# The first weight tile behind three norms computed before the norm's factor is known

## The chip, the cores and the metric

The kernel runs on one core of one Trainium2 chip. The metric is the device time of one execution in microseconds (us), median of three runs. A profile is taken of a further execution of the same program; its span runs from the first to the last instruction, and its device time is a little longer than the span.

## The reference, cut to what matters

Two decoder layers work on 256 tokens of width 1024. Layer 0 mixes tokens with dilated attention, layer 1 with gated linear attention (GLA); each is followed by a gated feed-forward part. Ahead of each of these four parts stands a norm that is modulated by a vector `c`:

```python
mod = jax.nn.silu(c) @ w_ada[i] + b_ada[i]
sh1, sc1, g1, sh2, sc2, g2 = [m[:, None, :] for m in jnp.split(mod, 6, axis=-1)]
h = rmsnorm(x, norm_mix[i]) * (1.0 + sc1) + sh1
x = x + g1 * y                                  # y: attention or GLA of h
h = rmsnorm(x, norm_ffn[i]) * (1.0 + sc2) + sh2
x = x + g2 * conv_ffn(h, w_up[i], conv_w[i], conv_b[i], w_down[i])
```

GLA takes from `h` the projections q, k (4 heads), v, a low-rank gate `glr` and an output gate r. From `glr` comes `gk = log_sigmoid(glr @ w_gate + b) / 16`, its running sum over chunks of 64 tokens, and three exponentials of that sum, which scale q and k before anything is done with them.

## The kernel before, in words

Activations are stored transposed: 8 tiles of 128 features by 256 tokens (`x`, and `h_hi`, `h_lo`). Every product is made in about full precision from two reduced parts of each operand: `mm3` (lines 171 to 176) issues hi·hi, hi·lo and lo·hi, so a weight tile of 2048 columns (a pair of 128-column blocks for 8 feature tiles) is 48 matmuls of 128 x 256. `split` (155 to 169) loads such a tile with one DMA of 1 MB on SyncE's queue, casts its two halves on ScalarE (`whi`, line 165) and subtracts them on VectorE (`wlo`, line 168). There are four raw buffers and three of each split part.

A norm is: `residual` (271) adds the last products to `x` on VectorE; `add_square` (195) squares on ScalarE and adds up; `rstd_of` (183) sums over features with three matmuls by a constant (line 186), then Ln and Exp on ScalarE (188, 190); `normed` (246) makes for each feature tile `x·(1+scale)·r` on VectorE (250), the hi part with the shift on ScalarE (252) and the lo part on VectorE (253). `all_normed` (265) does this for three of the four norms: ahead of the feed-forward part of layer 0, of GLA, and of the feed-forward part of layer 1. Between the sums and the first product it issues six small matmuls on constants (`keep_warm(6)`, line 263).

The modulation vectors are computed in 48 chunks: `ada_chunk` (129) loads 1 MB and reduces it in two VectorE instructions (138) to two columns of 128. Eight chunks belong to the first norm; the other 40 stand in the list `rest` and `next_ada()` takes the next one at places written into the loops.

`ffn` (541) runs 22 up-projection tiles (`pab`), each followed by a convolution over tokens and a gate, and then 32 down-projection tiles (`pd`). GLA first makes v (`pv`, four tiles), with the low-rank gate after the second (`log_gates`, 614): `glr` (621), four products `z` (625), `nz` (626), Abs, Exp and Ln on ScalarE (630 to 632), `sp` (634) and the running sum `cs` (637) on VectorE, `e_q` and `e_k` (641, 642), `dl` (644), `e_d` (646). Then `states(hd)` (673) for each head: 48 matmuls for q and k into one PSUM bank of the tag "p", of which there are two, then `k_d`, `q_t`, `k_t` (682 to 684) on VectorE, which need the exponentials, and then small matmuls on them (690, 696, 706).

The program is ordered by a scheduler that simulates a timeline; the order on each engine is then fixed. `behind(...)` keeps an instruction after another one on the same engine. Each engine issues strictly in this order.

Of the kernel before, what the change touches and what calls it, by code (L numbers as in the profile page):

```python
# [11 lines left out]
F32 = mybir.dt.float32  # L12
# [6 lines left out]
P = 128  # L19
# [38 lines left out]
def trunk(ctx: ExitStack, tc: tile.TileContext, I, out):  # L58
# [93 lines left out]

    last_load, copied, last_lo = [None], [None], [None]

    def split(src, n, dmas=1, after=((), ())):
        raw = wraw.tile([P, 2048], F32, tag="raw", name="raw")
        for i in range(dmas):
            c = slice(n * i // dmas, n * (i + 1) // dmas)
            last_load[0] = nc.sync.dma_start(raw[:, c], src[:, c])
        hi = wspl.tile([P, 2048], F32R, tag="whi", name="whi")  # L160
        lo = wspl.tile([P, 2048], F32R, tag="wlo", name="wlo")
        for i in range(0, n, n // 2):
            c = slice(i, i + n // 2)
            with behind(*after[i > 0]):
                copied[0] = nc.scalar.copy(hi[:, c], raw[:, c])  # L165
        for i in range(0, n, n // 2):
            c = slice(i, i + n // 2)
            last_lo[0] = nc.vector.tensor_tensor(lo[:, c], raw[:, c], hi[:, c].bitcast(F32), op=ALU.subtract)  # L168
        return hi, lo

    def mm3(ps, a, b, start, stop):
# [4 lines left out]
        return mm(ps, a[1], b[0], start=False, stop=stop)  # L176

    def hpart(name, dt, n=KT):
        return [state.tile([P, T], dt, tag=f"{name}{k}", name=name) for k in range(n)]

    norm_ops = []

    def rstd_of(squares, n=D, tag=None):
        ps = bank("ms", tag)
        for i, sq in enumerate(squares):
            a = mm(ps[:, :T], ones_d, sq, start=(i == 0), stop=(i == len(squares) - 1))
# [3 lines left out]
        norm_ops[:] = a, nc.scalar.activation(r, ln, AF.Exp, scale=-0.5)  # L190
        return r

    sums = {}

    def add_square(kt):

        sq = tmp.tile([P, T], F32, tag="sq", name="sq")
        i = nc.scalar.activation(sq, x[kt], AF.Square)
        part = 0 if kt < 3 else 1 if kt < 7 else 2
        if kt in (0, 3, 7):  # L200
            sums[part] = sq
        else:
            acc = tmp.tile([P, T], F32, tag="sqacc", name="sqacc")
            (nc.gpsimd if kt < 3 else nc.vector).tensor_tensor(acc, sums[part], sq, op=ALU.add)
            sums[part] = acc
        if kt < 6:
            squared[0] = i
# [38 lines left out]
    def normed(l, sub, r, kt):  # L246

        xr = tmp.tile([P, T], F32, tag="xr", name="xr")
        a, sh = mod[l, 3 * sub + 1, kt], mod[l, 3 * sub, kt]
        nc.vector.scalar_tensor_tensor(xr, x[kt], a[:, 0:1], r, op0=ALU.mult, op1=ALU.mult)  # L250
        hi, lo = h_hi[kt][:, :], h_lo[kt][:, :]
        i = nc.scalar.activation(hi, xr, AF.Identity, bias=sh[:, 0:1])  # L252
        j = nc.vector.scalar_tensor_tensor(  # L253
            lo, xr, sh[:, 0:1], hi.bitcast(F32), op0=ALU.add, op1=ALU.subtract
        )
        chain[kt] = chain[7] = i, j
        return h_hi[kt], h_lo[kt]

    def keep_warm(n):

# [1 line left out]
        for i in range(n):  # L262
            mm(ps[:, :P], ones_d, ones_d, start=True, stop=True)

    def all_normed(l, sub):
        r = rstd_of([sums[0], sums[1], sums[2]])
        with behind(norm_ops[0]):
            keep_warm(6)
        return [normed(l, sub, r, kt) for kt in range(KT)]

    def residual(l, sub, kt, ps):
        g = mod[l, 3 * sub + 2, kt]
        i = nc.vector.scalar_tensor_tensor(x[kt], ps, g[:, 0:1], x[kt], op0=ALU.mult, op1=ALU.add)
        if kt < 6:
            squared[1] = i

    def parts(w, at, n=P):
        return w[0][:, at : at + n], w[1][:, at : at + n]
# [49 lines left out]
    for kt in range(KT):  # L328
        with behind(*first):
            term = ada_chunk(0, kt, dmas=1 if kt else 2)  # L330
        h.append(normed(0, 0, r, kt))
        if kt:
            w0.append(split(I["w0"][kt], 15 * P))
        else:
            with behind(chain[0][1]):
                w0.append(split(I["w0"][kt], 15 * P, 2, after=((term,), (chain[0][0],))))
# [178 lines left out]
    def project(src, o, l, sub):  # L515

        ends = []
        for n in range(4):
            w = split(src[n], 2048)
            ps = [bank("py", "ppst"[n])] * 2  # L520
            if n == 3:
                ps[1] = bank("py", "s")
            order = [(kt, i) for kt in range(KT) for i in range(2)]
            if n == 3:
                order.sort(key=lambda x: x[1])
            for kt, i in order:
# [12 lines left out]
    last_pd = [None]  # L539

    def ffn(l):
        h = all_normed(l, 1)
        with tc.tile_pool(name=f"ffn{l}", bufs=2) as pool:
            g_hi = [pool.tile([P, T], F32R, tag=f"ghi{i}", name="ghi", bufs=1) for i in range(NFF)]
            g_lo = [pool.tile([P, T], F32R, tag=f"glo{i}", name="glo", bufs=1) for i in range(NFF)]
            for i in range(NFF):
                with behind(*(squared[:1], chain[3], chain[7])[min(i, 2)]):
                    w = split(I["w_up"][l, i], 2048)
                pab = bank("pab")
                pu = [pab[:, :T], pab[:, T:]]  # L550
                for kt in range(KT):
# [24 lines left out]
            for f2 in range(0, KT, 2):  # L576
                pd = [bank("pd") for _ in range(2)]
                for half, f in ((0, 0), (0, 1), (1, 0), (1, 1)):
                    w = split(I["w_down"][l, f2 + f, half], 11 * P)
                    for j in range(11):  # L580
                        i = 11 * half + j
                        last_pd[0] = mm3(pd[f][:, :T], parts(w, P * j), (g_hi[i], g_lo[i]), i == 0, i == NFF - 1)
                for f in range(2):
# [4 lines left out]
                    if l == 0 and f2 < 6:  # L588
                        next_ada()

    ffn(0)

# [57 lines left out]

    pv = [[bank("pv", tg) for _ in range(2)] for tg in "ps"]
    for n in range(4):
        with behind(*(squared, chain[5], chain[7], glr_copy)[n]):
            w = split(I["w_v_b"][n], 2048)
            if n > 1:
# [15 lines left out]
    o_n = []  # L671

    def states(hd):
        w = split(I["w_qk_b"][hd], 2048)
        pqk = bank("pqk", "p")
        pq, pk = pqk[:, :T], pqk[:, T:]
        for kt in range(KT):
            mm3(pq, parts(w, 2 * P * kt), h[kt], kt == 0, False)
            mm3(pk, parts(w, 2 * P * kt + P), h[kt], False, kt == KT - 1)
        c = slice(T * hd, T * hd + T)  # L680
        q_t, k_t, k_d = (gt([P, T], nm, bufs=2) for nm in ("q_t", "k_t", "k_d"))
        nc.vector.tensor_tensor(k_d, pk, e_d[:, c], op=ALU.mult)
# [80 lines left out]
    output(3, *s3)  # L763
    for n in range(1, 4):
        gate(n)
        if n < 2:
            next_ada()
    o = []
    for n in range(4):
        r = r_g[n // 2][:, 2 * (n % 2) : 2 * (n % 2) + 2, :]  # L770
# [156 lines left out]
```

## Time and profile before

| | |
|---|---|
| median of 3 runs | 803.75 us (802.86, 803.75, 808.61) |
| device time of the profiled execution | 802.44 us |
| its span | 800.7 us |
| mean granted clock of TensorE | 0.995 |
| TensorE busy | 781.9 us, 98% of the span |
| VectorE, ScalarE, GpSimd busy | 643.9, 468.2, 15.2 us |
| bytes moved | 184.72 MB |

In the views, PE is TensorE (PEld its weight loads), DVE VectorE, ACT ScalarE, POOL GpSimd, SP SyncE. A row of the timeline has start and duration in us, engine, line, operation, output<-input, and at its end the engine's idle time before it with what ended that. A row of the windows has the stretch, its length, the busy time of each engine with the number of instructions, the granted clock (PEclk), the DMA share and GB/s.

### The profile page before, as it was taken

How to read it: one execution, taken by the hardware profiler on the slowest of the kernel's cores; microseconds unless marked ns; L12 is line 12 of the kernel's file. 1: busy time of each engine (PE TensorE's matmuls, PEld its weight loads, DVE VectorE, ACT ScalarE, POOL GpSimd, SP SyncE). 2: the span in 40 equal slices, each digit the busy share in tenths (PEclk: the TensorE clock that was granted, in tenths of full speed). 3: DMA queues.
4: the chain of work that ended last, by engine and by line, in shares of the span. 5: the costliest groups of instructions: out<-in, count | busy, mean ns of one | idle time of the engine just before them, and what ended most of it. 6: DMA issues, size and time to landing. Idle time of an engine off the chain costs nothing.

```text
span 800.7 us, 15941 instructions
## 1 busy us (share of the span) xinstructions
PE 781.9 (98%) x6486; PEld 753.3 (94%) x6486; DVE 643.9 (80%) x1150; ACT 468.2 (58%) x869; POOL 15.2 (2%) x40
## 2 busy tenths in 40 slices
PE   7999999999999999999999999999999999999997
PEld 5999999999999989999999998889998999999997
DVE  6988978879778759999997877785468999988552
ACT  5556555555555546776765545744566866666442
POOL 1000000000000010000000100000010000000100
PEclk9899999999999999999999999999999999999999
DMA  8998577585685825886647793973343777644531
GB/s 343 418 334 298 202 280 278 202 329 197 248 312 200 301 85 204 301 301 223 240 162 249 268 332 127 366 261 108 106 156 109 275 269 248 251 141 159 181 110 53
DMA packets 32183, 184.72 MB, mean 231 GB/s; under 512 B 5804, under 2 KB 7340, under 8 KB 15470
## 3 DMA queue, kind: packets, MB, share of 16 engines
q1 hardware_dynamic: 32110, 183.70, 63.9%
q8 instruction: 51, 0.84, 0.4%
q14 instruction: 22, 0.18, 0.1%
HBM read 182.59 MB, written 1.10 MB: 229 GB/s over the span
## 4 chain that ended last, share of the span: by engine, by line
PE 89%; DVE 5%; DMA 3%; ACT 2%; issue 1%; SPq 0%; ACTq 0%; DVEq 0%
PE pab L176 10%; PE pab L175 10%; PE pab L174 10%; PE pqk L174 7%; PE pqk L175 6%; PE pqk L176 6%; PE pd L176 5%; PE pd L175 5%; PE pd L174 5%; PE pv L174 3%; PE pv L175 3%; PE pv L176 3%; DVE wlo L168 2%; PE py L175 2%; PE py L174 2%; PE s L367 2%
## 5 line engine op out<-in xcount | busy, mean ns | idle before, releaser
L168 DVE TENSOR_TENSOR wlo<-raw,whi 128x1024 fp32r<-128x1024 f32 (+2 forms) x274 | 295.8, 1107 | 55.6 <-ACT whi L165 54.8
L165 ACT CAST whi<-raw 128x1024 fp32r<-128x1024 f32 (+2 forms) x274 | 248.1, 954 | 152.4 <-PE pab L175 50.6
L174 PE MATMUL pab<-hhi,whi 128*128 128x256 f32 x704 | 194.0, 277 | 1.5 <-ACT hhi L252 1.5
L175 PE MATMUL pab<-hlo,whi 128*128 128x256 f32 x704 | 193.9, 276 | 0.5 <-DVE hlo L253 0.5
L176 PE MATMUL pab<-hhi,wlo 128*128 128x256 f32 x704 | 194.0, 276 | 0.4 <-DVE wlo L168 0.4
L174 PEld LDWEIGHTS pab<-hhi,whi 128*128 128x128 f32 x704 | 132.0, 188 | 2.2 <-ACT hhi L252 1.9
L175 PEld LDWEIGHTS pab<-hlo,whi 128*128 128x128 f32 x704 | 132.0, 188 | 0.9 <-DVE hlo L253 0.9
L176 PEld LDWEIGHTS pab<-hhi,wlo 128*128 128x128 f32 x704 | 132.0, 188 | 0.8 <-DVE wlo L168 0.8
L174 PE MATMUL pqk<-hhi,whi 128*128 128x256 f32 x448 | 123.5, 287 | 3.7 <-ACT hhi L252 3.2
L175 PE MATMUL pqk<-hlo,whi 128*128 128x256 f32 x448 | 125.0, 283 | 0.0
L176 PE MATMUL pqk<-hhi,wlo 128*128 128x256 f32 x448 | 124.9, 283 | 0.0
L138 DVE CUSTOM_DVE_ANT_0 ada_raw<-ada_raw,c_bc 128x1024 f32<-128x1024 f32 x96 | 113.5, 1218 | 4.5 <-DMA ada_raw<-in_w_ada 4.4
L176 PE MATMUL pd<-ghi,wlo 128*128 128x256 f32 x352 | 98.0, 280 | 0.6 <-DVE wlo L168 0.6
L175 PE MATMUL pd<-glo,whi 128*128 128x256 f32 x352 | 98.1, 280 | 0.0
L174 PE MATMUL pd<-ghi,whi 128*128 128x256 f32 x352 | 97.7, 279 | 0.0
L174 PEld LDWEIGHTS pqk<-hhi,whi 128*128 128x128 f32 x448 | 83.7, 191 | 5.5 <-ACT hhi L252 3.7
L175 PEld LDWEIGHTS pqk<-hlo,whi 128*128 128x128 f32 x448 | 85.0, 190 | 0.4
L176 PEld LDWEIGHTS pqk<-hhi,wlo 128*128 128x128 f32 x448 | 84.9, 190 | 0.2
L176 PEld LDWEIGHTS pd<-ghi,wlo 128*128 128x128 f32 x352 | 65.8, 187 | 0.8 <-DVE wlo L168 0.8
L175 PEld LDWEIGHTS pd<-glo,whi 128*128 128x128 f32 x352 | 66.0, 188 | 0.0
L174 PEld LDWEIGHTS pd<-ghi,whi 128*128 128x128 f32 x352 | 65.9, 188 | 0.0
L560 ACT ACTIVATE r<-pab,small 128x256 f32<-128x256 f32 x88 | 48.5, 559 | 11.7 <-DVE r L563 11.3
(184 smaller groups left out, 1248.2 us busy)
## 6 DMA issues: line engine op xcount, KB each, us to landing
ada_raw<-in_w_ada SPq DMA_DIRECT2D x47, 1024.0 KB, 6.7
raw<-in_w_up SPq DMA_DIRECT2D x44, 1024.0 KB, 5.2
raw<-in_w_down SPq DMA_DIRECT2D x32, 704.0 KB, 4.2
raw<-in_wqk SPq DMA_DIRECT2D x18, 1024.0 KB, 7.2
raw<-in_wv SPq DMA_DIRECT2D x14, 768.0 KB, 4.6
raw<-in_w SPq DMA_DIRECT2D x7, 960.0 KB, 6.6
raw<-in_w_out_a SPq DMA_DIRECT2D x4, 1024.0 KB, 6.9
raw<-in_w_v_b SPq DMA_DIRECT2D x4, 1024.0 KB, 6.7
```

What stands on the lines that cost most here:

```text
L138: nc.vector.tensor_tensor_reduce(w, w, c_bc, op0=ALU.mult, op1=ALU.add, scale=1.0, scalar=0.0, accum_out=dot,)
L165: copied[0] = nc.scalar.copy(hi[:, c], raw[:, c])
L168: last_lo[0] = nc.vector.tensor_tensor(lo[:, c], raw[:, c], hi[:, c].bitcast(F32), op=ALU.subtract)
L174: mm(ps, a[0], b[0], start=start, stop=False)
L175: mm(ps, a[0], b[1], start=False, stop=False)
L176: return mm(ps, a[1], b[0], start=False, stop=stop)
L367: mm(s[:, 0:n], q[0][a][:, r].rearrange("p a b -> p (a b)"), k[0][b][:, 0:n], start=(i == 0), stop=(i == 2))
L560: nc.scalar.activation(r, u[:, :T], AF.Identity, scale=cw[2], bias=col(C_CB + 44 * l + f))
```

## The change

With r the norm's factor per token, `h = x·(1+scale)·r + shift`. So a product of a weight with h is r times the product with `x·(1+scale)`, plus the product with the shift, which is the same for every token. After the change the first weight tile behind each of the three norms is multiplied with `x·(1+scale)`, and the shift stands in a 257th column (a 258th is zero) of the same operand. When r is there, `whole` multiplies 256 columns of the sums by r and adds the 257th.

For this, `scale(l, sub, kt)` writes hi and lo parts of `x·(1+scale)` into the tiles that later hold h, right after each residual (one instruction on ScalarE, one on VectorE for each feature tile); `shift_columns` writes the shift's two parts (eight instructions of one column on each of the two engines, for each norm); the h tiles grow by 32 columns, cleared at the start on GpSimd. The products of the first two feature tiles go ahead of the sums over features, the other six behind them, in the place of `keep_warm(6)`. In the feed-forward parts this tile is the first of the up-projection; at GLA it is q and k of head 0, kept in `qk0`, so that `states(0)` has no product of its own. The second weight tile is split at chosen places of the norm.

Modulation chunks move: in the up-projections 6 become 3 (layer 0) and 4 become 0 (layer 1); the v loop has 3 instead of 2, the gates 4 instead of 2, and the down-projection of layer 1 has 4 instead of 0. In all they stay 40.

```diff
+    def shift_columns(l, sub):
+        for kt in range(KT):
+            hi, lo = (z[kt][:, T : T + 1] for z in (h_hi, h_lo))
+            with behind(*chain[7]):
+                nc.scalar.copy(hi, mod[l, 3 * sub, kt])
+                nc.vector.tensor_tensor(lo, mod[l, 3 * sub, kt], hi.bitcast(F32), op=ALU.subtract)
+
+    def scale(l, sub, kt):
+        a, hi, lo = mod[l, 3 * sub + 1, kt], h_hi[kt][:, 0:T], h_lo[kt][:, 0:T]
+        i = nc.scalar.activation(hi, x[kt], AF.Identity, scale=a[:, 0:1])
+        j = nc.vector.scalar_tensor_tensor(lo, x[kt], a[:, 0:1], hi.bitcast(F32), op0=ALU.mult, op1=ALU.subtract)
+        scaled[kt] = i, j
...
-    def all_normed(l, sub):
-        r = rstd_of([sums[0], sums[1], sums[2]])
+    def all_normed(l, sub, tags, second):
+        ps = [bank("early", t) for t in tags]
+        def products(tiles):
+            for kt in tiles:
+                for s in range(2):
+                    mm3(ps[s][:, 0:TS], parts(early[0], 2 * P * kt + P * s), (h_hi[kt][:, 0:TS], h_lo[kt][:, 0:TS]),
+                        kt == 0, kt == KT - 1)
+        products(range(2))
+        r = rstd_of([sums[0], sums[1], sums[2]], tag="p")
         with behind(norm_ops[0]):
-            keep_warm(6)
-        return [normed(l, sub, r, kt) for kt in range(KT)]
+            products(range(2, KT))
+        def whole(s, out):
+            dot = tmp.tile([P, 1], F32, tag="dot", name="dot", bufs=4)
+            nc.scalar.copy(dot, ps[s][:, T : T + 1])
+            nc.vector.tensor_tensor(out, ps[s][:, 0:T], r, op=ALU.mult)
+            nc.scalar.activation(out, out, AF.Identity, bias=dot[:, 0:1])
+            return out
+        h = [normed(l, sub, r, kt) for kt in range(KT)]
+        early[1] = split(second, 2048, after=(scaled[6][:1], chain[0][:1], last_x, chain[2][1:]))
+        return h, whole
...
     def project(src, o, l, sub):
+        shift_columns(l, 1)
...
+            if n == 3:
+                with behind(*scaled[3]):
+                    early[0] = split(I["w_up"][l, 0], 2048)
             for i in range(2):
                 residual(l, sub, 2 * n + i, ps[i][:, T * i : T * i + T])
                 add_square(2 * n + i)
+                scale(l, 1, 2 * n + i)
...
     def ffn(l):
-        h = all_normed(l, 1)
+        h, whole = all_normed(l, 1, "st", I["w_up"][l, 1])
...
-                if i % (3, 5)[l] == 2 and i < 20:
-                    with behind(*chain[7]):
+                if l == 0 and i % 7 == 3:
+                    with behind(last_lo[0]):
                         next_ada()
...
+                    if l == 1 and (half, f) == (0, 0):
+                        next_ada()
...
-    h = all_normed(1, 0)
+    h, whole = all_normed(1, 0, "tt", I["w_v_b"][0])
...
     for n in range(4):
+        if n == 0:
+            w = early[1]
+            with behind(*chain[7]):
+                qk0 = gt([P, 2, T], "qk0")
+                for s in range(2):
+                    whole(s, qk0[:, s, :])
+        else:
+            with behind(*((), chain[5], chain[7], glr_copy)[n]):
+                w = split(I["w_v_b"][n], 2048)
+            with behind(last_lo[0]):
                 next_ada()
...
     def states(hd):
+        if hd == 0:
+            pq, pk = qk0[:, 0, :], qk0[:, 1, :]
+        else:
+            w = split(I["w_qk_b"][hd], 2048)
...
     for n in range(1, 4):
         gate(n)
-        if n < 2:
-            next_ada()
+        next_ada()
```

More of the change, by code (lines that the diff above doesn't have):

```diff
@@ L153, in trunk, with split @@
     last_load, copied, last_lo = [None], [None], [None]
-    def split(src, n, dmas=1, after=((), ())):
+    def split(src, n, dmas=1, after=((), (), (), ())):
         raw = wraw.tile([P, 2048], F32, tag="raw", name="raw")
@@ L167, in split @@
             c = slice(i, i + n // 2)
-            last_lo[0] = nc.vector.tensor_tensor(lo[:, c], raw[:, c], hi[:, c].bitcast(F32), op=ALU.subtract)
+            with behind(*after[2 + (i > 0)]):
+                last_lo[0] = nc.vector.tensor_tensor(lo[:, c], raw[:, c], hi[:, c].bitcast(F32), op=ALU.subtract)
         return hi, lo
@@ L178, in hpart @@
     def hpart(name, dt, n=KT):
-        return [state.tile([P, T], dt, tag=f"{name}{k}", name=name) for k in range(n)]
+        return [state.tile([P, T + 32], dt, tag=f"{name}{k}", name=name) for k in range(n)]
     norm_ops = []
@@ L191, in rstd_of @@
         return r
-    sums = {}
+    sums, last_sum, last_x = {}, [], []
     def add_square(kt):
@@ L203, in add_square @@
             acc = tmp.tile([P, T], F32, tag="sqacc", name="sqacc")
-            (nc.gpsimd if kt < 3 else nc.vector).tensor_tensor(acc, sums[part], sq, op=ALU.add)
+            last_sum[:] = [(nc.gpsimd if kt < 3 else nc.vector).tensor_tensor(acc, sums[part], sq, op=ALU.add)]
             sums[part] = acc
@@ L250, in normed @@
         nc.vector.scalar_tensor_tensor(xr, x[kt], a[:, 0:1], r, op0=ALU.mult, op1=ALU.mult)
-        hi, lo = h_hi[kt][:, :], h_lo[kt][:, :]
+        hi, lo = h_hi[kt][:, 0:T], h_lo[kt][:, 0:T]
         i = nc.scalar.activation(hi, xr, AF.Identity, bias=sh[:, 0:1])
@@ L256, in normed @@
         chain[kt] = chain[7] = i, j
-        return h_hi[kt], h_lo[kt]
+        return h_hi[kt][:, 0:T], h_lo[kt][:, 0:T]
+    TS = T + 2
+    for z in h_hi + h_lo:
+        nc.gpsimd.memset(z[:, T:].bitcast(F32), 0.0)
+    early, scaled = {}, {}
+    def shift_columns(l, sub):
[9 more added lines that the diff above has]
+        scaled[kt] = i, j
     def keep_warm(n):
@@ L263, in keep_warm @@
             mm(ps[:, :P], ones_d, ones_d, start=True, stop=True)
-    def all_normed(l, sub):
-        r = rstd_of([sums[0], sums[1], sums[2]])
-        with behind(norm_ops[0]):
-            keep_warm(6)
-        return [normed(l, sub, r, kt) for kt in range(KT)]
+    def all_normed(l, sub, tags, second):
[7 more added lines that the diff above has]
+        r = rstd_of([sums[0], sums[1], sums[2]], tag="p")
+        with behind(norm_ops[0]):
+            products(range(2, KT))
[8 more added lines that the diff above has]
+        return h, whole
     def residual(l, sub, kt, ps):
         g = mod[l, 3 * sub + 2, kt]
-        i = nc.vector.scalar_tensor_tensor(x[kt], ps, g[:, 0:1], x[kt], op0=ALU.mult, op1=ALU.add)
+        with behind(*(last_sum if kt == 7 else ())):
+            i = nc.vector.scalar_tensor_tensor(x[kt], ps, g[:, 0:1], x[kt], op0=ALU.mult, op1=ALU.add)
         if kt < 6:
             squared[1] = i
+        last_x[:] = [i]
     def parts(w, at, n=P):
@@ L335, in trunk @@
             with behind(chain[0][1]):
-                w0.append(split(I["w0"][kt], 15 * P, 2, after=((term,), (chain[0][0],))))
+                w0.append(split(I["w0"][kt], 15 * P, 2, after=((term,), (chain[0][0],), (), ())))
             with behind(copied[0]):
@@ L546, in ffn @@
             for i in range(NFF):
[L547 to L551, printed above, removed]
+                w = early.get(i)
+                if i > 1:
+                    with behind(*chain[7]):
+                        w = split(I["w_up"][l, i], 2048)
+                if i == 0:
+                    with behind(*chain[7]):
+                        pu = [whole(s, pool.tile([P, T], F32, tag="u", name="u")) for s in range(2)]
+                else:
+                    pab = bank("pab")
+                    pu = [pab[:, :T], pab[:, T:]]
+                for kt in range(KT if i else 0):
                     for s in range(2):
@@ L576, in ffn @@
             for f2 in range(0, KT, 2):
+                if (l, f2) == (0, 4):
+                    shift_columns(1, 0)
                 pd = [bank("pd") for _ in range(2)]
@@ L582, in ffn @@
                         last_pd[0] = mm3(pd[f][:, :T], parts(w, P * j), (g_hi[i], g_lo[i]), i == 0, i == NFF - 1)
+                if (l, f2) == (0, 6):
+                    with behind(*scaled[3]):
+                        early[0] = split(I["w_qk_b"][0], 2048)
                 for f in range(2):
@@ L587, in ffn @@
                         nc.scalar.mul(x[f2 + f], x[f2 + f], col(C_NFIN + f2 + f))
-                    if l == 0 and f2 < 6:
-                        next_ada()
+                    if l == 0:
+                        scale(1, 0, f2 + f)
+                        if f2 < 6:
+                            next_ada()
     ffn(0)
@@ L652, in trunk @@
     for n in range(4):
-        with behind(*(squared, chain[5], chain[7], glr_copy)[n]):
-            w = split(I["w_v_b"][n], 2048)
-            if n > 1:
+        if n == 0:
+            w = early[1]
+            with behind(*chain[7]):
+                qk0 = gt([P, 2, T], "qk0")
[5 more added lines that the diff above has]
+            with behind(last_lo[0]):
                 next_ada()
@@ L673, in states @@
     def states(hd):
[L674 to L679, printed above, removed]
+        if hd == 0:
+            pq, pk = qk0[:, 0, :], qk0[:, 1, :]
+        else:
+            w = split(I["w_qk_b"][hd], 2048)
+            pqk = bank("pqk", "p")
+            pq, pk = pqk[:, :T], pqk[:, T:]
+            for kt in range(KT):
+                mm3(pq, parts(w, 2 * P * kt), h[kt], kt == 0, False)
+                mm3(pk, parts(w, 2 * P * kt + P), h[kt], False, kt == KT - 1)
         c = slice(T * hd, T * hd + T)
@@ L765, in trunk @@
         gate(n)
-        if n < 2:
-            next_ada()
+        next_ada()
     o = []
```

## The prediction

> **What bounds the kernel now.** I read the page's first part, then the windows of single stages, then the waits of PE, then the timeline where those waits stand.
>
> ```profile
> span 800.7 us, 15941 instructions
> PE 781.9 (98%) x6486; PEld 753.3 (94%) x6486; DVE 643.9 (80%) x1150; ACT 468.2 (58%) x869; POOL 15.2 (2%) x40
> ```
>
> PE is the bound; 18.8 us of the span are its idle time. The device time of this execution is 802.44 us, 1.74 more than the span and 1.31 below the median of the three runs, 803.75. Three windows show how full the stages are (up-projection and down-projection of layer 0, the output projection of layer 1):
>
> ```profile
> 310.00:420.00 110.00, 110.00 (x973) 110.00 (x972) 106.86 (x186) 78.87 (x138) 0.00 (x0) 1.00 0.71 252
> 422.00:485.00 63.00, 62.44 (x530) 62.23 (x530) 47.57 (x75) 31.59 (x55) 2.23 (x2) 1.00 0.81 288
> 585.00:605.00 20.00, 20.00 (x179) 20.00 (x178) 12.85 (x22) 11.04 (x19) 2.08 (x2) 1.00 0.43 152
> ```
>
> The up-projection has no hole: one matmul each 113 ns (110.00/973), a tile of 48 in 5.4 us. DVE is 97% full there, yet PE never waits for it, so taking modulation chunks out of that stage gains nothing. The down-projection runs at 118 ns (62.44/530) with matmuls of the same shape; I come back to this. The output projection leaves DVE 7 of 20 us free. So the change can only gain where PE stands: around the norms.
>
> ```profile
> 297.45 1.03 PE L186 MATMUL ms<-sqacc,ones_d 128*128 128x256 f32 x4
> 298.69 0.70 PE L186 MATMUL ms<-sq,ones_d 128*128 128x256 f32 x2 [0.22 <-ACT sq L198]
> ...
> 299.94 0.42 ACT L190 ACTIVATE rstd<-ln 128x256 f32<-128x256 f32 x1
> 300.39 1.28 DVE L250 SCALAR_TENSOR_TENSOR xr<-x_all,mod,rstd 128x256 f32<-128x256 f32 x3 [2.26 <-ACT rstd L190]
> ...
> 301.58 0.88 DVE L253 SCALAR_TENSOR_TENSOR hlo<-xr,mod,hhi 128x256 fp32r<-128x256 f32 x2
> ```
>
> From the first sum at 297.45 PE does 1.73 us of sums, then warming matmuls and waits until the first h tile at 301.47. The windows of its products from there tell how slowly they begin (the first of the feed-forward part, the second of GLA's v, whose sums start at the time of the third row):
>
> ```profile
> 301.47:306.00 4.53, 4.08 (x29) 3.54 (x29) 0.00 (x0) 0.00 (x0) 1.00 0.00 0
> ...
> 489.48:494.50 5.02, 5.01 (x22) 4.14 (x23) 0.00 (x0) 0.00 (x0) 1.00 0.01 3
> ```
>
> ```profile
> 485.52 1.03 PE L186 MATMUL ms<-sqacc,ones_d 128*128 128x256 f32 x4
> ```
>
> Feed-forward norm: 306.00 - 297.45 = 8.55 us, less 1.73 of sums, less 29 x 0.113 = 3.3 of products: 3.5 us lost. The norm of layer 1 has the same form, 3.5. GLA: 489.48 - 485.52 - 1.73 = 2.2, and from then on PE is full (22 products at 228 ns). In all 9.2 us: the most that the change can gain.
>
> One more wait matters, because the change moves work around it: PE waits in GLA until the exponentials of the gate have scaled k.
>
> ```profile
> 509.35 1.99 PE L625 MATMUL z<-glr,w_g 16*128 16x256 f32 x8
> ...
> 510.89 1.99 ACT L165 CAST whi<-raw 128x1024 fp32r<-128x1024 f32 x2
> ...
> 516.70 1.07 ACT L632 ACTIVATE ea<-ea 128x1024 f32<-128x1024 f32 x1
> 517.80 1.23 DVE L634 SCALAR_TENSOR_TENSOR sp<-nz,ea 128x1024 f32<-128x1024 f32 x1 [0.26 <-ACT ea L632]
> 518.95 1.22 DVE L168 TENSOR_TENSOR wlo<-raw,whi 128x1024 fp32r<-128x1024 f32 x1
> 520.08 2.28 DVE L637 TENSOR_TENSOR_SCAN cs<-keep,sp 128x1024 f32<-128x1024 f32 x1
> 522.40 1.06 ACT L641 ACTIVATE e_q<-cs 128x1024 f32<-128x1024 f32 x1 [2.75 <-DVE cs L637]
> 524.54 1.22 DVE L138 CUSTOM_DVE_ANT_0 ada_raw<-ada_raw,c_bc 128x1024 f32<-128x1024 f32 x1
> 526.83 2.35 DVE L168 TENSOR_TENSOR wlo<-raw,whi 128x1024 fp32r<-128x1024 f32 x2
> ...
> 529.10 0.41 DVE L682 TENSOR_TENSOR k_d<-pqk,e_d 128x256 f32<-128x256 f32 x1
> 529.57 0.44 PE L690 MATMUL kdt<-ident,k_d 128*128 128x128 f32 x2 [1.44 <-DVE k_d L682]
> 530.23 0.71 PE L696 MATMUL a<-q_t,k_t 128*128 128x128 f32 x4 [0.22 <-DVE k_t L684]
> ```
>
> The chain from `z` to `k_d` takes 19.75 us. Meanwhile PE has the rest of v and the products of two heads (96 matmuls), which fill both PSUM banks of the tag "p"; then it stands for 1.44 and 0.22 us. This chain is covered to within 1.7 us, with nothing to spare.
>
> **The change part by part.** The order that the changed program is built with is fixed, so I use it for what stands where.
>
> *Feed-forward norms.* Twelve early products go ahead of the sums: 1.4 us, longer than the residual and the square need, so the sums no longer wait. After the sums follow 36 products, 4.1 us. The factor r comes about 1.0 us after the last sum (rows 298.69 and 299.94: 300.36 - 299.39). What is late next is h for the second tile: h may only be written when r is there, and from then to the end of that tile's products there are 4.1 + 5.4 - 1.0 = 8.5 us, in which DVE has 16 norm instructions at 0.43 (1.28/3, 0.88/2), 6.9 us, the second half of this tile's wlo and both of the next one's at 1.2 each: 10.5 us. So 2.0 of the 3.5 us remain as waits for hlo and wlo; gain 1.5 for each of the two norms (bounds 0 and 3.5: the order may let DVE hold up everything, or nothing).
>
> *GLA's norm.* The v products take 12 x 0.228 = 2.7 us for each feature tile, DVE 0.9; no wait is left: gain 2.2 (lower bound 1). Sum of the three norms 5.2 (1 to 9.2).
>
> *Added work.* `scale` adds per norm 8 instructions to ACT and to DVE, nearest row hlo, 0.44: 3.5 us each. Their cover is the idle DVE of the projections ahead (7 of 20 us; 15 of 63). Without that cover each would come in front of a residual; that is a rival below. Shift columns, `whole`, clearing at the start (POOL is busy 2%): nothing on PE's path; above nothing by the same cover. Early products have 258 columns instead of 256:
>
> ```profile
> L367 PE MATMUL s<-k,q 128*128 128x258 f32 x48 | 10.4, 315 | 0.0
> L367 PE MATMUL s<-k,q 128*128 128x256 f32 x24 | 5.4, 292 | 0.0
> ```
>
> By columns 144 x 1 ns = 0.1 us, by these means 144 x 23 ns = 3.3; the means mix in what follows each, so I take 0.2.
>
> *The gate's chain.* Head 0's products are made at the norm, so PE's cover behind `z` is now the rest of v and heads 1 and 2: again 96 matmuls in the two "p" banks, no more. But the chain gets longer. On DVE a second modulation chunk stands between `sp` and `cs` (2.3 us: 526.83 - 524.54), and `q_t`, `k_t` are issued ahead of `k_d` (0.7). On ACT four more weight casts stand between `nz` and the Ln, since the splits now run one head further ahead: 2 x 1.99 = 4.0 us, and some column copies, 0.2. Sum 7.2. ACT sits idle only behind the Ln (2.75 before `e_q`), so casts ahead of it aren't hidden. Bounds: 2.3 if all ACT work fell into gaps, 9 if a chunk's load also delays a weight in the full DMA queue:
>
> ```profile
> 500.00:510.00 10.00, 10.00 (x55) 8.43 (x54) 7.64 (x10) 4.88 (x7) 0.00 (x0) 1.00 0.96 381
> ```
>
> PE stands 1.7 + 7.2 = 8.9 us in one piece at `a`; behind it in PE's order wait all other heads and the gates, whose work is then done later, not saved.
>
> *The clock.* The trace shows once what a hole does:
>
> ```profile
> 21.63 1.01 PE L174 MATMUL pqk<-hhi,whi 128*128 128x256 f32 x3 [2.70 <-ACT hhi L252]
> ```
>
> ```profile
> 20.00:21.00 1.00, 0.00 (x0) 0.00 (x0) 1.00 (x3) 0.00 (x0) 0.00 (x0) 0.95 0.93 385
> 21.00:24.00 3.00, 2.37 (x9) 2.37 (x10) 3.00 (x7) 2.30 (x4) 0.00 (x0) 0.50 1.02 423
> ...
> 27.00:28.00 1.00, 1.00 (x7) 1.00 (x7) 1.00 (x3) 0.57 (x2) 0.00 (x0) 0.63 1.03 418
> ```
>
> After 2.70 us without work the granted clock is 0.50 from 20.9 to 27.7, 6.1 us of it after work is back: half of that, 3.1 us, is lost if PE is dense, half as much if it is mostly waiting on short chains as behind `a`. I take 2.4 (0 if the hole stays short). The Trainium skill, "TensorE: Matmul & The Clock Gate", Part 1, says that one idle window of about 3.4 us halves the clock and one busy window of that length restores it, windows running freely. The row agrees in kind; by the rule alone the return would cost 1.7 us instead of 2.4. It also speaks against the change where `keep_warm` goes, but there the 36 products keep PE busy.
>
> *Moved chunks* elsewhere stay under PE: in the down-projection of layer 1 DVE has room as in layer 0 (47.57 of 63).
>
> Sum: -5.2 + 7.2 + 2.4 + 0.2 = +4.6 us on 802.44: **807.0 us**.
>
> **The rivals.**
>
> *A. The gain arrives, the hole doesn't grow.* Casts and chunk slip into waits of the chain that are there anyway (before `sp` 0.26, before `e_q` 2.75). Then 802.44 - 9.2 + 2.3 = 795.5. For it: ACT is busy only 58%. Against it: the row of `e_q` has its slack behind the Ln, not ahead.
>
> *B. The up-projections fall to the slower pace.* The same matmul takes 113 ns in one stage and 118 in another, at a granted clock of 1.00 in both, so something that the stages' rows don't name sets it. The up-projection now follows early products instead of a halt, and reads h tiles 1152 bytes apart. If its 42 remaining tiles ran at 118: 2016 x 4.7 ns = 9.5 us, 816.5; one layer alone 811.7. It decides with the first tile behind each norm. Against it: both layers ran at 113.
>
> *C. The early block is late itself.* If `scale` delays the residual, the square or the wlo of the early tile, PE waits ahead of the block as it did behind the sums, and the norms gain nothing: 807.0 + 5.2 = 812.2. For it: two DVE instructions more for each pair of output tiles, in front of the last wlo. Against it: DVE's free time in those projections.
>
> **How the numbers follow.** Forecast 0.55, A 0.12, B 0.20, C 0.13. The forecast's own range is 802 to 812 (its bounds without the extremes together). The whole range goes to 799, which keeps the near half of A, and to 816, B in nearly both layers. About 1% is what a measurement of this kernel tells from no change, 8 us: 795.7 to 811.8. Faster by more is half of A, 0.06. Slower by more is three quarters of B, half of C and the forecast's upper end (0.04): 0.26. The rest, 0.68, is within 1%.
>
> **What would show each step.** Right: no warming matmuls, 48 early products for each norm with no wait over 0.3 us among them; waits of 1 to 2.5 us for hlo and wlo in the second and third tiles; PE waiting 7 to 10 us for `k_t` or `k_d`, a granted clock of 0.50 after it; two reductions between `sp` and `cs`. Wrong: a wait under 3 us there (A), 118 ns in the up-projections (B), waits ahead of the early products (C).

## The result, and the profile after

The changed kernel takes 814.09 us (median of 7 runs, 810.79 to 816.19) against 803.75: a ratio of 1.0125, 95% interval 1.0103 to 1.0146. A second comparison later gave 1.0123 (1.0104 to 1.0142). It is slower by 10 us. The prediction said 807.0, 799 to 816: the sign and the range held, the sum was 7 us too small by the medians. The time lies above the forecast's own range of 802 to 812, and the prediction had put 0.68 on a change within 1%. The profiled execution took 811.51 us, 9.07 more than that of before (802.44); the terms below are held against this difference, of which +4.6 was forecast.

The page's first part, with the idle time of PE now 24.8 us of the span:

```profile
span 809.7 us, 16040 instructions
PE 784.9 (97%) x6450; PEld 757.2 (94%) x6450; DVE 660.0 (82%) x1204; ACT 483.3 (60%) x929; POOL 16.0 (2%) x56
```

PE is idle 6 us longer, and busy 3 us longer with 36 matmuls fewer. Both halves need a cause. The waits of PE (time in total, times, longest) name the first:

```profile
PE a L769 <- DVE k_t L757: 8.8, 1, 8.8
PE pd L177 <- DVE wlo L169: 1.6, 1, 1.6
PE pab L177 <- DVE wlo L169: 1.0, 2, 0.5
PE pab L176 <- DVE hlo L254: 0.5, 2, 0.2
```

One stall of 8.8 us stands out, at `a`, the small matmuls of `q_t` and `k_t`; in the tiles behind the norms 1.5 us is left in all (the rows of `pab`). The timeline of the chain that ends in it:

```profile
515.82 1.99 PE L688 MATMUL z<-glr,w_g 16*128 16x256 f32 x8
...
528.17 1.23 DVE L697 SCALAR_TENSOR_TENSOR sp<-nz,ea 128x1024 f32<-128x1024 f32 x1 [0.64 <-ACT ea L695]
529.31 1.22 DVE L138 CUSTOM_DVE_ANT_0 ada_raw<-ada_raw,c_bc 128x1024 f32<-128x1024 f32 x1
...
530.45 1.22 DVE L138 CUSTOM_DVE_ANT_0 ada_raw<-ada_raw,c_bc 128x1024 f32<-128x1024 f32 x1
...
532.74 2.28 DVE L700 TENSOR_TENSOR_SCAN cs<-keep,sp 128x1024 f32<-128x1024 f32 x1
...
542.63 1.22 PE L769 MATMUL a<-q_t,k_t 128*128 128x128 f32 x4 [8.83 <-DVE k_t L757]
```

From `z` to `a` it takes 26.8 us, 20.9 before; both reductions of a chunk lie between `sp` and `cs`. The second half shows in windows of PE alone (busy time and instructions, granted clock, DMA share, GB/s), two in the up-projections of the two layers, one in a down-projection:

```profile
320.00:420.00 100.00, 100.00 (x863) 1.00 0.62 220
640.00:720.00 80.00, 80.00 (x692) 1.00 0.56 193
745.00:785.00 40.00, 40.00 (x342) 1.00 0.70 239
```

An up-projection matmul now takes 116 ns (100/863, 80/692) where it took 113, at full clock and without a wait; the down-projection is unchanged at 117 to 118. So half of rival B came true, in both layers. From the starts of successive matmuls a tile of 48 takes 5.57 us instead of 5.44, and within a tile the two paces alternate: products of four of the eight feature tiles follow each other at 118 ns, those of the other four at 113 to 116. That is what the experiments began with.

Where the stages begin in the changed kernel: each row of the timeline is the first early product, the first down-projection product (`pd`) or the first product of the output projection (`py`):

```profile
297.66 0.28 PE L175 MATMUL early<-hhi,whi 128*128 128x258 f32 x1
424.10 0.28 PE L175 MATMUL pd<-ghi,whi 128*128 128x256 f32 x1
488.20 0.28 PE L175 MATMUL early<-hhi,whi 128*128 128x258 f32 x1
591.66 0.28 PE L175 MATMUL py<-ohi,whi 128*128 128x256 f32 x1
613.90 0.28 PE L175 MATMUL early<-hhi,whi 128*128 128x258 f32 x1
739.39 0.28 PE L175 MATMUL pd<-ghi,whi 128*128 128x256 f32 x1
```

Four rows of the kernel before close the account with those shown ahead (297.45 and 485.52 for its first sums there):

```profile
422.51 0.28 PE L174 MATMUL pd<-ghi,whi 128*128 128x256 f32 x1
582.75 0.28 PE L174 MATMUL py<-ohi,whi 128*128 128x256 f32 x1
605.26 1.03 PE L186 MATMUL ms<-sqacc,ones_d 128*128 128x256 f32 x4
730.32 0.28 PE L174 MATMUL pd<-ghi,whi 128*128 128x256 f32 x1
```

Norm and up-projection of layer 0: 126.4 instead of 125.1 (+1.4); of layer 1: 125.5 instead of 125.1 (+0.4). Down-projection of layer 0: 64.1 instead of 63.0 (+1.1). All of GLA up to its output projection: 103.5 instead of 97.2 (+6.2). The rest -0.1. Together the span's 9.0.

### The profile page after: what moved, and what is told of

It reads as the page before. It is cut to its first block, busy times and chain, and to the rows that moved or that the text cites. A ratio compares the mean times of both kernels' runs of the same rounds, so it can differ in the third digit from the quotient of the medians.

```text
span 809.7 us, 16040 instructions
## 1 busy us (share of the span) xinstructions
PE 784.9 (97%) x6450; PEld 757.2 (94%) x6450; DVE 660.0 (82%) x1204; ACT 483.3 (60%) x929; POOL 16.0 (2%) x56
## 4 chain that ended last, share of the span: by engine, by line
PE 82%; DVE 8%; DMA 5%; ACT 2%; issue 2%; SPq 0%; DVEq 0%; ACTq 0%
PE pab L176 9%; PE pab L177 9%; PE pab L175 9%; PE pqk L175 6%; PE pqk L176 6%; PE pqk L177 6%; PE pd L177 4%; PE pd L176 4%; PE pd L175 4%; DVE wlo L169 3%; PE pv L175 3%; PE pv L176 3%; PE pv L177 3%; DMA ada_raw<-in_w_ada 2%; PE s L410 2%
## 5 line engine op out<-in xcount | busy, mean ns | idle before, releaser
L169 DVE TENSOR_TENSOR wlo<-raw,whi 128x1024 fp32r<-128x1024 f32 (+3 forms) x274 | 294.8, 1106 | 55.6 <-ACT whi L165 55.2
L165 ACT CAST whi<-raw 128x1024 fp32r<-128x1024 f32 (+3 forms) x274 | 247.9, 954 | 146.2 <-PE pab L176 47.0
L176 PE MATMUL pab<-hlo,whi 128*128 128x256 f32 x672 | 187.5, 279 | 0.5 <-DVE hlo L254 0.5
L177 PE MATMUL pab<-hhi,wlo 128*128 128x256 f32 x672 | 186.6, 278 | 1.0 <-DVE wlo L169 1.0
L175 PE MATMUL pab<-hhi,whi 128*128 128x256 f32 x672 | 186.8, 278 | 0.0
L177 PEld LDWEIGHTS pab<-hhi,wlo 128*128 128x128 f32 x672 | 125.8, 187 | 1.4 <-DVE wlo L169 1.4
L176 PEld LDWEIGHTS pab<-hlo,whi 128*128 128x128 f32 x672 | 126.2, 188 | 0.9 <-DVE hlo L254 0.9
L175 PEld LDWEIGHTS pab<-hhi,whi 128*128 128x128 f32 x672 | 126.2, 188 | 0.0
L175 PE MATMUL pqk<-hhi,whi 128*128 128x256 f32 x432 | 119.1, 287 | 3.0 <-ACT hhi L253 2.6
L177 PE MATMUL pqk<-hhi,wlo 128*128 128x256 f32 x432 | 120.3, 283 | 0.0
```

Source lines behind the costliest of these rows:

```text
L175: mm(ps, a[0], b[0], start=start, stop=False)
L176: mm(ps, a[0], b[1], start=False, stop=False)
```

## The experiments

A tile's *place* is here its byte address within a partition, modulo 256, as the built program lays it out. In the kernel before, every h tile lies at 224 and every g tile (the operand of the down-projection) at 96. The weight tiles lie at 32 in every version. The change makes h tiles 1152 bytes long, so that they lie at 224 and 96 in turn.

**The change's 32 columns alone, in the kernel before.**

```
-    return [state.tile([P, T], dt, ...
+    return [state.tile([P, T + 32], dt, ...
```

> The kernel before, with its sixteen h tiles allocated 32 columns wider (1152 bytes apart instead of 1024), as in the changed kernel; the extra columns are never touched, and the order of instructions is that of before. Theory (pace by the place of the moving tile): the four h tiles of each kind that then lie 96 bytes past a multiple of 256 are read at 118 ns a matmul, those at 224 stay near 114, so an up-projection tile of 48 takes 5.57 us instead of 5.44; 44 tiles x 0.13 = 5.7 us, plus up to 2 us in GLA and attention, whose products read the same tiles: 809 to 812 against a before of 803.75. Rival (the pace comes from how the stage begins, early products instead of a halt): tiles stay at 5.44, within 1 us of before.

809.8 us against 803.47, a ratio of 1.0088 (1.0068 to 1.0108). Its windows of the same two up-projections:

```profile
320.00:420.00 100.00, 100.00 (x864) 1.00 0.69 242
640.00:720.00 80.00, 80.00 (x691) 1.00 0.61 217
```

Same instructions in the same order, no early products, and the pace of the changed kernel (864 and 691 beside 863 and 692). The start of the stage, which I had put first under rival B, is out as the cause of this loss; the distance between the tiles, which I had put second, is what does it. More than half of the loss (6.3 of 10) comes from columns of which the change uses two.

**All h tiles at 224, or all at 96, in the changed kernel.**

```
-    return [state.tile([P, T + 32], dt, ...
+    return [state.tile([P, T + 64], dt, ...
-                qk0 = gt([P, 2, T], "qk0")
+                qk0 = gt([P, 2, T], "qk0", tag="on0")
 and for 96, on top of it, around the h tiles:
-    shift(state, 16)
+    shift(state, 48)
```

> The changed kernel with h tiles 64 columns wider instead of 32 (1280 bytes apart, so that all sixteen lie 224 bytes past a multiple of 256, as in the kernel before); qk0 shares its place with on0 to make room. Theory (pace by place): tiles of the up-projections back at 5.44 us, early products nearer 113 than 120 ns; 42 x 0.13 + 0.9 = 6 us less than the changed kernel: about 808 by medians. Rival (start of the stage): tiles stay at 5.57, 814. The stall of about 9 us at a stays by both.

> As the kernel with h tiles 1280 bytes apart, but all of them 128 bytes further, so that every one lies 96 bytes past a multiple of 256. Theory (pace by place): every up-projection matmul at 118 ns, a tile 5.65 us; against the kernel with all at 224 42 x 0.21 = 9 us more, against the changed kernel 3 to 4 us more: about 817. Rival (distance between tiles, or the start of the stage, and not the place): as the kernel with all at 224.

810.28 us (ratio 1.0081, 1.0049 to 1.0114) and 817.35 us (1.0182, 1.0158 to 1.0206). The window 320:420 of the one, then of the other:

```profile
320.00:420.00 100.00, 100.00 (x885) 1.00 0.64 227
```

```profile
320.00:420.00 100.00, 100.00 (x851) 1.00 0.62 219
```

113 and 117.5 ns. With the distance the same in both, the place remains. The whole steps were 7.1 us between the two (9 expected) and about 4 from the changed kernel to the first (6 expected). In the first one's trace the stages from the early products to the down-projection take 123.8 and 122.8 us, 5.4 less than in the changed kernel, as expected of the pace. The 0.9 us that I had hoped for in the early products did not come: a product with 258 columns takes 120.9 ns with h at 224, 119.5 to 120.0 in the changed kernel. GLA took 0.6 us more there. As the weight tiles stay at 32, these runs do not tell the place itself from the distance between the moving tile and the weights.

**The same on the down-projection, in the kernel before.**

```
+            shift(pool, 16)
             g_hi = [pool.tile([P, T], F32R, ...
             g_lo = [pool.tile([P, T], F32R, ...
+            shift(pool, 16)
```

> The kernel before with one small unused tile ahead of the g tiles of the feed-forward part and one behind them, so that g lies 224 instead of 96 bytes past a multiple of 256. The order of instructions is the same. Theory (pace by place): the down-projections fall from 118 to 113 ns a matmul, 2 x 528 x 4.7 ns = 5 us less: 798.8 against 803.75. Rival (something else in the down-projection, its weights of 1408 columns or its two banks, sets 118): within 1 us of before.

799.28 us, a ratio of 0.9952 (0.9936 to 0.9967): two unused tiles make the kernel 4 us faster (5 expected). The window in the down-projection of layer 1, beside the 342 of the changed kernel for the same g at 96:

```profile
745.00:785.00 40.00, 40.00 (x356) 1.00 0.32 111
```

112.4 ns. The open point of the prediction, why matmuls of the same shape took 113 in one stage and 118 in another, is answered as far as the place goes.

**GLA's norm put back, and the chunk taken from its chain.** Two versions of the changed kernel, h tiles left as in it.

```
 the first: scale(1, 0, ..), its shift columns, qk0 and the early split removed
-    h, whole = all_normed(1, 0, "tt", I["w_v_b"][0])
+    h = plain_normed(1, 0)        # sums, keep_warm(6), normed, as before
 the second, in v's loop, where n is 1, 2, 3:
+            if n > 1:
                 with behind(last_lo[0]):
                     next_ada()
 both, so that as many chunks are made:
-                if l == 0 and i % 7 == 3:
+                if l == 0 and i % 5 == 3:
```

> The changed kernel with the norm of GLA as before (sums first, warming matmuls, head 0's products behind v), and with the modulation chunks in v's loop as before; the one chunk left over goes to the up-projection of layer 0. The two feed-forward norms stay in two parts and the h tiles 1152 bytes apart. Theory (early head 0 and the chunk lengthen the gate's chain): the stall at a falls from 8.8 to below 3 us, no half clock there, minus 7 and minus 1.4; the norm gives back 2.9: 5.5 us less than the changed kernel, a ratio to before of 1.0055. Rival (the hole only moves work that is waited for later, so its end is what counts): within 2 us of the changed kernel, 1.0125.

> The changed kernel with one modulation chunk fewer in v's loop (none with its second pair of tiles) and one more in the up-projection of layer 0. Nothing else changes. Theory (the chunk between sp and cs is 2.3 us of the stall, and two weight casts that now come behind the Ln another 2): the stall at a falls from 8.8 to 4 to 6.5 us and the half clock to at most 2 us: 3 to 5 us less than the changed kernel, a ratio to before of 1.007 to 1.009. Rival (the splits alone set the stall, the chunk fills waits): stall 8 to 9, no change, 1.0125.

They took 807.04 and 812.06 us in one comparison. The kernel before took 802.9 to 813.6 there, for a reason that a later run makes likely, so the two are held against each other and by their stages, not by the ratio. GLA put back, from its first sum to the output projection:

```profile
488.48 0.81 PE L187 MATMUL ms<-sqacc,ones_d 128*128 128x256 f32 x3
585.87 0.28 PE L175 MATMUL py<-ohi,whi 128*128 128x256 f32 x1
```

97.4 us, that of before (97.2) and 6.1 less than the changed kernel. So the whole +6.2 of this stage belongs to the norm in two parts and to the chunks around it: the rival, by which the hole only moves time, is out. The time, 807.0, is near the 808 that the expected ratio gives on 803.75.

The moved chunk shortens the stall less than expected. Its waits of PE in that stage:

```profile
PE kdt L764 <- DVE k_d L756: 4.0, 1, 4.0
PE kv L780 <- ACT kdT L765: 1.2, 1, 1.2
PE a L770 <- DVE k_t L758: 0.4, 1, 0.4
```

8.8 us have become 5.6, in three pieces; the longest is there because DVE now does another pair of wlo and a chunk between `k_t` and `k_d`. The stage lasts 102.2 us, only 1.3 less. The clock accounts for most of the difference. In windows of 1 us, the changed kernel (stall 533.8 to 542.6), then this one (534.9 to 538.9):

```profile
538.00:539.00 1.00, 0.00 (x0) 0.89 0.84 352
539.00:540.00 1.00, 0.00 (x0) 0.50 1.06 451
...
544.00:545.00 1.00, 1.00 (x7) 0.50 1.13 410
545.00:546.00 1.00, 1.00 (x8) 0.69 0.85 287
```

```profile
538.00:539.00 1.00, 0.15 (x1) 0.74 0.81 336
539.00:540.00 1.00, 0.60 (x3) 0.50 1.04 442
...
544.00:545.00 1.00, 1.00 (x5) 0.50 0.72 287
545.00:546.00 1.00, 1.00 (x7) 0.84 0.98 401
```

From the shares of the first and the last window (0.89 is full clock for 0.78 us, 0.69 for 0.38) half clock lasts 538.78 to 545.62 in the one and 538.48 to 545.32 in the other: 6.84 us both times. In the changed kernel PE stood for most of it and worked 3.0 us at half speed (1.5 lost); with the shorter stall it worked 6.1 us at half speed (3.0 lost). Of 3.2 us saved at the waits, 1.5 went back to the clock. The expected 3 to 5 us had counted on at most 2 us of half clock.

This price is not fixed, though. A second traced execution of the changed kernel (described below) has the same stall, and its half clock begins at 538.74, as here, but PE comes back 1.0 us later:

```profile
543.67 0.58 PE L769 MATMUL a<-q_t,k_t 128*128 128x128 f32 x1 [8.82 <-DVE k_t L757]
```

```profile
538.00:539.00 1.00, 0.00 (x0) 0.87 0.86 139
...
548.00:549.00 1.00, 1.00 (x6) 0.51 1.19 336
```

There half clock lasts 10.24 us, to 548.98, of which PE worked 5.3 (2.7 lost, and a stage of 104.5 us). So part of what the moved chunk lost to the clock is how the return of work fell in these two executions. The Trainium skill, "TensorE: Matmul & The Clock Gate", Part 1, has the clock judged in free-running windows of 3413 ns; 6.84 us is two of them and 10.24 us three, and the traces agree.

**The versions that put these together.** The first is the changed kernel with GLA put back, h tiles 1280 bytes long and g moved; the second keeps GLA's norm in two parts and has the moved chunk.

> The changed kernel with GLA's norm and chunks as before, h tiles 1280 bytes apart and g moved by 128 bytes, so that both lie 224 bytes past a multiple of 256. Theory: the feed-forward norms in two parts gain 2 us each against before, the down-projections 5, the early products cost 0.6, up-projections at 5.44 a tile: 795 to 798 against 803.5, a ratio of 0.991. Rival (the early part gains nothing by itself): as the kernel before with g moved, 0.995.

> The changed kernel with the moved chunk, h tiles 1280 bytes apart and g moved by 128 bytes; GLA's norm stays in two parts. Theory: against the changed kernel minus 6 (h), minus 5 (g), minus 4 (stall): 799, a ratio to before of 0.995; it stays behind the version with GLA's norm as before by 2 to 4 us, since the stall at a still costs more than the norm's 2.9 us. Rival (the stall nearly goes with the chunk): 0.990 or better.

> The version with the feed-forward norms in two parts, GLA as before, h tiles 1280 bytes apart and g moved by 128 bytes, on the same chip as before and the changed kernel: 797 to 801, 0.98 to 0.985 of the changed kernel, 0.986 to 0.995 of before.

799.72 and 803.36 us in the comparison above: with h and g at the same places, GLA's norm in two parts costs 3.6 us even with the chunk moved. The order of the two was as expected. The second missed its 799: its trace has the wait of 4.0 us for `k_d` again, and one of 2.8 us for `wlo` in the down-projection of layer 0. In a later comparison the first took 797.1 against 803.1 of before, a ratio of 0.9925 (0.9899 to 0.9951), and against 812.6 of the changed kernel in the same comparison 0.981. It beats both. Its two feed-forward stages begin and end so:

```profile
297.30 0.28 PE L175 MATMUL early<-hhi,whi 128*128 128x258 f32 x1
421.06 0.28 PE L175 MATMUL pd<-ghi,whi 128*128 128x256 f32 x1
...
603.68 0.28 PE L175 MATMUL early<-hhi,whi 128*128 128x258 f32 x1
726.46 0.28 PE L175 MATMUL pd<-ghi,whi 128*128 128x256 f32 x1
```

123.8 and 122.8 us, each with its h tiles at 224 and at 113 ns, as the 125.1 of before: this is the norm in two parts, with fewer modulation chunks in these stages, by itself: 1.3 and 2.3 us.

**Before and after once more, with a trace.**

> The kernel before, unchanged, with a trace of its own: in the comparison with the last four kernels it took 810.5 us (802.9 to 813.6), 7 more than in the others, at a granted clock of 0.996 to 0.998. Theory (h tiles at 224 can be read at 113 or at 118, and an execution can fall into the slow pace for a whole stage): an execution of 808 us or more shows 118 ns in an up-projection and no longer wait than before. Rival (memory or a longer wait): 113 ns in both up-projections and the time in waits. An execution of 802 to 804 leaves it open.

> The changed kernel, unchanged, beside before and the best version on one chip. Half of its h tiles lie at 96 and are always read at 118, so by the theory of places it varies less than the kernel before: 811 to 816. Rival: it is slower by the same share wherever it runs, 1.0125 of before.

Before: 802.58 us (798.8 to 809.8); after: 812.6 us (811.3 to 813.9). The traced execution of before took 804.75, not the 808 that I had asked for, but its windows tell the two theories apart all the same:

```profile
320.00:420.00 100.00, 100.00 (x851) 1.00 0.69 238
640.00:720.00 80.00, 80.00 (x708) 1.00 0.65 225
```

The same program, h at 224 throughout: 117.5 ns in layer 0, 113 in layer 1. So at 224 a stage can run at either pace; at 96 it ran at 118 in every trace here. This accounts for 4.6 us of one traced execution.

Where the pace changes shows in the first trace of the best version, in its down-projection of layer 0 with g at 224: a window ahead of a wait of PE, the row of that wait, and a window behind it.

```profile
423.00:439.00 16.00, 16.00 (x144) 1.00 0.79 299
```

```profile
441.72 0.38 PE L177 MATMUL pd<-ghi,wlo 128*128 128x256 f32 x1 [1.34 <-DVE wlo L169]
```

```profile
446.00:483.00 37.00, 37.00 (x316) 1.00 0.82 299
```

By the starts of successive matmuls it is 113.3 ns ahead of the wait and 117.8 behind it. A stretch is here a run of over 100 up- or down-projection matmuls with no halt in it. All traces together have 27 stretches with every moving tile at 224: 19 ran at 113 from end to end and 8 at 118, and the pace changed only across a halt. All 29 stretches with every tile at 96 ran at 118. So at 224 how a stretch begins does count, which was the first cause named under rival B; what decides it at a halt is open. It is also why the best version's down-projections brought less than the 5 us expected of them: that of layer 0 took 63.0 us in this trace, as before.

The traced execution of the best version in the later comparison was its slowest, 807.03 us where the others took 794.0 to 803.4:

```profile
320.00:420.00 100.00, 100.00 (x851) 1.00 0.64 227
640.00:720.00 80.00, 80.00 (x682) 1.00 0.54 184
```

Both up-projections ran at 117 to 118 ns, and their stages took 127.6 and 127.0 us instead of 123.8 and 122.8: 8.1 of the 9.6 us between the spans of the two traced executions of this version. That the pace explains the whole spread of before (799 to 814) is likely and not shown.

**Two more places.** The best version with h at 0 and g at 32.

```
-    shift(state, 16)      ahead of h; behind it 72
+    shift(state, 24)
-            shift(pool, 16)      ahead of g; behind it 12
+            shift(pool, 20)
```

> The best version with its tiles in two places not tried yet: h at a multiple of 256 itself (0), g 32 bytes past one. Theory (a matmul can run at 113 only where its moving tile lies in the upper half of 256 bytes): h and g both at 118, an up-projection tile 5.65 us, a down-projection 62.1: 797 + 42 x 0.21 + 5 = 811, and little spread. Rival (only some places such as 96 are bad): both stages at 113 in at least some executions, 792 to 800. If h and g differ, the place decides in finer steps than halves.

814.93 us (813.4 to 817.2): 15 to 18 us more than the best version, for tiles moved by 32 and 64 bytes. Its windows in an up-projection and a down-projection:

```profile
320.00:420.00 100.00, 100.00 (x847) 1.00 0.64 228
745.00:785.00 40.00, 40.00 (x336) 1.00 0.72 242
```

118 and 119 ns by the counts. Successive starts stand 120 ns apart throughout with g at 32 and vary from 115 to 123 with h at 0. Neither place is fast, as the theory of halves had it, but the paces are 118 (at 96), 120 (at 32) and uneven (at 0): finer than halves. How the place comes to matter is open; no run here tells a mechanism.

## Why the prediction was right or wrong

| step | forecast, us | measured in the profile, us | from |
|---|---|---|---|
| feed-forward norms | -3.0 | -3.6 | the best version's stages against before |
| two more columns in early products | +0.2 | in the norms | |
| norm of GLA | -2.2 | -2.4 | by subtraction: what is left of the stage's +6.2 |
| stall at `a` | +7.2 | +7.1 | 8.8 less the 1.66 of before |
| half clock behind it | +2.4 | +1.5 | 3.0 us of work at 0.50; 2.7 lost in the second trace |
| pace of the up-projections | 0 | +5.4 | 126.4 - 123.8 and 125.5 - 122.8 |
| down-projection, layer 0 | 0 | +1.1 | the stage |
| sum | +4.6 | +9.1 | spans +9.0, times +9.07 |

*The norms* went as forecast: no warming matmuls, 48 products with no wait over 0.3 us, short waits for `wlo` and `hlo` behind. The waits were even shorter (0.7 for each norm instead of 2.0), but the early products run at about 120 ns, not at the 114 that 0.2 us for all columns allowed; that is in the -3.6.

*The gate's chain* was right in the size of the stall, 8.8 against 8.9, and in its two large parts: from `sp` to `cs` it is 4.6 us (532.74 - 528.17), 2.3 more than before, and from `z` to `sp` 12.35 (528.17 - 515.82) instead of 8.45, the four casts. But the whole chain from `z` to `a` grew by 5.9 us and not by 7.2. PE's own work in it was forecast as unchanged and fell from 19.2 us (20.9 less the waits of 1.66) to 18.0 (26.8 less 8.8). The two misses cancel, so that the stall came out to 0.1 us is luck. GLA put back removed it.

*The clock* was right in kind; 1.5 instead of 2.4, since the first 3.8 us of the half clock fell into the stall itself. The forecast had it last 6.1 us behind the return of work, as after the shorter hole of before. The second trace of the changed kernel shows 2.7 and the run with the moved chunk 3.0; all lie between 0 and 3.1. The prediction quotes from the Trainium skill, "TensorE: Matmul & The Clock Gate", Part 1, an idle window of about 3.4 us; the hole of 2.70 us that halved the clock in its row is shorter, so the row agrees with that only in part, and the row decides.

*The pace* is the step that failed: the sum put the up-projections at an unchanged 113 ns, that is at nothing, and they cost +5.4, more than the whole miss of 4.5. I named it as rival B, with its two possible causes, and priced it all or nothing: 118 ns in all matmuls of one layer or of both, 811.7 or 816.5. It was half of the matmuls in both layers. That the measured 814.09 lies within the whole range is owed to this rival, for which the range reached up to 816, and not to the sum. Its "against" was one trace in which both layers ran at 113; the second trace of before shows 118 in one of them, so that argument was worth little. And the profile held what would have raised its chance: the down-projection's constant 118. I noted it and left it open; had I set g's place beside h's, the new distance of 1152 bytes would have put half of the h tiles where g lies. Beside that, a chance of 0.20 looks too low.

*The down-projection of layer 0* has a wait for `wlo` of 1.6 us, where before has one of 0.6, and took 1.1 us more. The work moved there, forecast as covered, is not shown to be its cause: with GLA put back neither `scale` nor the early split of head 0 stands there, and the wait is 1.7; with all h tiles at 224 or at 96 that work stands there, in the same order, and the wait is 0.9. Its cause stays open. Rival C did not happen: no wait ahead of an early block is over 0.3 us. Nor did rival A.

## What to carry to other kernels

Look at where a matmul's moving tile lies before changing its length: here 32 columns of padding cost 6 us, and two unused tiles (64 bytes in each of two buffers) gained 4, with the order of the instructions unchanged. Pad so that the place modulo 256 stays, and compare two stages of one shape by ns per matmul. And before work is brought forward past a chain that PE's work only just covers, add up what lengthens that chain: here a chunk and four casts came into it, it grew by 5.9 us, and the early head gained 2.4 us for 8.6.

## What the runs showed of the hardware

At a granted clock of 1.00 throughout, a 128x256 fp32r matmul of these streams took 113 or 118 ns with its moving tile at 224 modulo 256 (one of the two from one halt of PE to the next, not always the same one for the same program), 118 at 96, 120 at 32, and 115 to 123 at 0. The half clock lasted 6.84 us behind a stall of 8.8 us and behind one of 4.0, and 10.24 us behind the same 8.8 in a second execution. Its price was set by how much of it PE spent working: the 8.8 us paid 1.5 and 2.7 us for it, the 4.0 paid 3.0.
